# A two-layer transformer block on one core: squares summed elementwise on VectorE, small TensorE products issued in groups of four

## The chip, the core and the metric
The kernel runs on one core of a Trainium2 chip. Its time is device microseconds of one execution. Three runs of the kernel before took 1551.24, 1543.52 and 1548.08 us, so the median is 1548.08.

## The reference, cut to what matters
A sequence of 512 tokens of width 1024 goes through two layers. Layer 0 has a mixer of two kinds of attention and a dense feed-forward. Layer 1 has a mixer of sparse attention and eight experts. Every mixer and every feed-forward reads a normalized x, scaled and shifted by a modulation, and its result is multiplied by a third modulation before it is added to x:

```python
sh_m, sc_m, g_m, sh_f, sc_f, g_f = ada_modulation(c, ada_w, ada_b)   # six rows of 1024 from silu(c) @ ada_w
h = rms_norm(x, norm_mix) * (1 + sc_m) + sh_m
x = x + g_m * mix
h = rms_norm(x, norm_ffn) * (1 + sc_f) + sh_f
logits = (t @ router_w).astype(jnp.float32) + router_b     # layer 1: 8 experts, the best two of each token
```

rms_norm needs, for every token, the sum of the squares of its 1024 features.

## The kernel before, in words
x is held as xT: features on the partitions, 8 tiles (k) of [128, 512 tokens]. All is float32. Large products are made of three products of rounded parts (mm3, lines 306 to 308): a weight block is loaded into a raw tile by SP's queue (wraw, line 288), rounded by ScalarE (line 297, wh) and the rest is taken by VectorE (line 299, wl). In the mixers there are three tiles of each kind. An instruction order is made by a planner from the program, by its own estimates of cost; each engine then runs its queue in that order.

Four places compute a norm. The first is at the very start, from the loaded xT. The other three are inside down, the products that end a mixer or a feed-forward: layer 0's output product (eout, from 248 us), the second half of layer 0's feed-forward (edn, from 626 us) and layer 1's output product (oout, from 914 us). down makes one feature tile of x at a time (24 or 30 products), updates xT by VectorE (line 496), and hands the tile before it to Norms.add. ScalarE squares it (line 417). For k below 6 TensorE sums the square over its 128 partitions by a product with a [128, 32] tile of ones, into one of four quarters of a bank (line 420); the quarters are copied, transposed and reduced at k = 5 and 6 (lines 423, 428, 430). The last two squares are summed by token directly: the square is the stationary operand and a column of ones moves (line 433). rstd ends with rsqrt_of.

Two more things are multiplied in small pieces. ada makes one modulation from 16 products [128, 32] x [128, 512] of a column of silu(c), spread over 32 columns, with a weight block (line 346): all products of a column group go to the same quarter of the bank, two blocks of weights make a pair of k-tiles. It runs twice: for modulation 1 of layer 0 at the start, with loads into tiles of its own, and for modulation 2 inside the first mixer, as a generator that is advanced by `fill(later, NA)` behind each of the first pieces of attention, through wraw's tiles. The other modulations are summed by VectorE (ada_vector, lines 368 and 370) and need TensorE only for the sum over partitions (line 374). During layer 0's output product, VectorE sums modulations 3 and 4 in this way, five steps for each tile, from loads in SP's queue. In layer 1's output product logits(k) adds a tile's part of the router's logits (line 1039), one product for each k, in the quarter k % 4. Layer 0's feed-forward and the experts are not touched.

Of the kernel before, what the change touches and what calls it, by code (L numbers as in the profile page):

```python
# [19 lines left out]
P = 128  # L20
# [22 lines left out]
# ---------------------------------------------------------------- host layout  # L43

def _tiles(w, nk, nc):
    """[K, N] -> [K/(nk*128), N/nc, 128, nk*nc], one contiguous block for each tile."""
    k, n = w.shape
    a = w.reshape(k // (nk * P), nk, P, n // nc, nc).transpose(0, 3, 2, 1, 4)
    return a.reshape(k // (nk * P), n // nc, P, nk * nc)


def _in_blocks(w, widths):
    """[1024, N] -> flat blocks for each column group: [128, 8*width], or two [128, 4*width] for a wide one."""
# [7 lines left out]
def _runs(nk):  # L61
    """Runs of k-tiles that share a block of a product with nk of them."""
    if nk <= 8:
        return [nk]
    return [-(-nk // 2), nk // 2]


def _down_blocks(w, groups):
    """[K, 1024] -> flat blocks: for each row group, each 128 columns, each run of k-tiles."""
# [11 lines left out]
def _gate_up_blocks(g, u):  # L81
    """Two [1024, N] -> column groups of 128, in turn gate and up."""
# [5 lines left out]
def _expert_blocks(g, u):  # L88
    """Two [1024, 1408] -> for each column group of THIRDS, each pair of k-tiles, gate and up: [128, 2*width]."""
# [11 lines left out]
def _ada_blocks(w):  # L101
    """[1024, 6144] -> [3 groups of 2048 columns][4 pairs of k-tiles][4 x 512 columns] blocks [128, 2*512]."""
# [53 lines left out]
# ---------------------------------------------------------------- the kernel  # L156
# [8 lines left out]
NA = 2  # L165
# [4 lines left out]
class Blocks:  # L170
    """Hands out consecutive blocks of [128, n] from a flat DRAM array [1, length]."""
# [10 lines left out]
def build(tc, I, out, dbg=None, stop=99):  # L182
# [19 lines left out]
    def temps(n):  # L202
        """The [128, 512] scratch tiles of a phase."""
# [8 lines left out]
    def prob_tiles(n):  # L212
        """The tiles of a phase for the exponentials of the scores."""
# [17 lines left out]
    def banks(**tags):  # L231
        """The PSUM banks of a phase: how many for each use."""
# [5 lines left out]
    # ---- inputs that everything waits for  # L238
# [10 lines left out]
    # ---- constants  # L249
# [21 lines left out]
    # tri[k, q] = 1 for q >= k  # L271
# [4 lines left out]
    # ---- streaming of weights  # L276
# [3 lines left out]
    def weights(raw, high, low):  # L280
        """The tiles of a phase for loaded weights, their high and their low parts."""
# [9 lines left out]
    def wkeep(blocks, nk, ncol):  # L291
        """The next block of weights, [128, nk, ncol]: (loaded, high, low)."""
# [17 lines left out]
    # ---- adaLN modulation  # L310
# [6 lines left out]
    def ada_blocks(layer, which):  # L317
        """The blocks of one of the six modulations: its two column groups' pairs of k-tiles."""
# [3 lines left out]
    def ada_columns(pt, layer, which):  # L322
        """The sums of the column groups of modulations, each on its 32 partitions, to their columns."""
        n = 2 * len(which)
# [5 lines left out]
        pc = pc.rearrange("p (b g r) -> p g b r", b=4, g=n)[:, :, :, 0]  # L330
        for i, w in enumerate(which):
            m = mods[layer, w] = cst.tile([P, KT], F32, name=f"mod{layer}{w}")
            v = V_ADA + 48 * layer + 8 * w
            V.tensor_add(m.rearrange("p (g b) -> p g b", b=4), pc[:, 2 * i:2 * i + 2],
                         vec[:, v:v + 8].rearrange("p (g b) -> p g b", b=4))

    def ada(layer, which, load=wraw, tag="mm"):
        """One of the six modulations, [128, 8]; a generator with a step for each load."""
        src = ada_blocks(layer, which)
        pt = bank(tag, "ada")  # L340
        for kp in range(4):
            for g in range(2):
                raw = load(src(g, kp), 1024)
                for j in range(2):
                    k = 2 * kp + j
                    T.matmul(pt[32 * g:32 * g + 32, :], cb[:, k], raw[:, j * 512:(j + 1) * 512], start=k == 0,
                             stop=k == KT - 1, tile_position=(0, 32 * g))
                yield
# [1149 lines left out]
```

## Time and profile before
| | |
|---|---|
| runs, us | 1543.52, 1548.08, 1551.24 |
| span of the profiled execution, us | 1543.3 |
| mean granted TensorE clock | 0.979 |
| TensorE busy | 1462.0 us, 95% |
| VectorE busy | 1038.0 us, 67% |
| ScalarE busy | 744.3 us, 48% |
| ones-products of the squares (line 420) | 24, in 48 instructions, 24.2 us busy |
| products of ada (line 346) | 32, in 64 instructions, 23.3 us busy |
| router products (line 1039) | 8, in 16 instructions, 7.2 us busy |

The profile is of one execution, and all times in it are microseconds from the start of its span. Nothing is shown of that execution's time outside the span. A float32 product stands in the trace as two matmul instructions. An engine's busy time does not say that it sets the end; the chain of waits does, and the busy time of a single stage.

### The profile page before, as it was taken

The page shows a single profiled execution, that of the slowest core. Times are in us where ns is not written, and L with a number is a line of the kernel's source. Part 1 is how long each engine was busy: PE and PEld are TensorE (multiplying, and loading weights), DVE is VectorE, ACT ScalarE, POOL GpSimd, SP SyncE. Part 2 cuts the span into 40 slices and gives each one's busy share as a digit, 9 for nine tenths or more (in the row PEclk, how much of TensorE's full clock was granted, in tenths as well). Part 3 has the DMA queues.
Part 4 walks back from the last instruction along what each step waited for, and adds up shares of the span by engine and source line. Part 5 has one row for each costly group of instructions (what it writes and reads, how often), then busy time and mean ns, then how long its engine had stood idle before and what let it go on. Part 6 is the DMA issues. An engine that isn't in the chain of part 4 may idle for free.

```text
span 1543.3 us, 23799 instructions
## 1 busy us (share of the span) xinstructions
PE 1462.0 (95%) x8659; PEld 1088.3 (71%) x8659; DVE 1038.0 (67%) x1968; ACT 744.3 (48%) x1252; POOL 149.9 (10%) x165
## 2 busy tenths in 40 slices
PE   7999999999999999999976999999999999999994
PEld 3766776677788878767854676776767777777773
DVE  5845577766574357347899852686677897897784
ACT  5444463332222222235444851665555675675672
POOL 1000000011110001003552000101100100010010
PEclk9999999999999999999998999999999999999997
DMA  8443325466674346333241101676878898798791
GB/s 313 147 129 104 102 84 181 173 205 211 194 233 154 109 129 211 90 96 90 81 116 40 42 28 56 245 252 206 289 234 275 289 367 249 269 386 247 265 390 59
DMA packets 84606, 283.26 MB, mean 184 GB/s; under 512 B 10488, under 2 KB 11272, under 8 KB 84480
## 3 DMA queue, kind: packets, MB, share of 16 engines
q1 hardware_dynamic: 70608, 233.87, 44.6%
q0 software_dynamic: 13872, 47.78, 10.4%
q8 instruction: 70, 1.15, 0.3%
q14 instruction: 56, 0.46, 0.1%
HBM read 261.28 MB, written 11.29 MB: 177 GB/s over the span
## 4 chain that ended last, share of the span: by engine, by line
PE 77%; DVE 9%; DMA 3%; issue 2%; ACT 2%; SPq 0%; POOL 0%; DVEq 0%; ACTq 0%; POOLq 0%
PE pj L306 6%; PE pj L308 6%; PE pj L307 6%; PE dn L306 5%; PE dn L307 5%; PE dn L308 5%; PE v L1310 4%; PE g L1303 3%; PE u L1304 3%; PE u L1303 3%; PE g L1305 3%; PE u L1305 3%; PE g L1304 3%; PE o L658 2%; DMA side<-in_oada 2%
## 5 line engine op out<-in xcount | busy, mean ns | idle before, releaser
L297 ACT CAST wh<-raw 128x1024 fp32r<-128x1024 f32 (+2 forms) x404 | 398.9, 993 | 459.8 <-PE dn L307 127.4
L299 DVE TENSOR_TENSOR wl<-raw,wh 128x1024 fp32r<-128x1024 f32 (+2 forms) x394 | 448.7, 1150 | 161.7 <-ACT wh L297 156.6
L306 PE MATMUL pj<-h,wh 128*128 128x512 f32 x560 | 225.4, 404 | 3.3 <-ACT h L457 3.2
L308 PE MATMUL pj<-h,wl 128*128 128x512 f32 (+1 forms) x560 | 224.1, 401 | 0.1
L307 PE MATMUL pj<-h,wh 128*128 128x512 f32 (+1 forms) x560 | 223.2, 399 | 0.1
L370 DVE SCALAR_TENSOR_TENSOR acc<-side,sc,acc 128x512 f32<-128x512 f32 x140 | 103.5, 750 | 46.2 <-DMA side<-in_oada 39.8
L306 PEld LDWEIGHTS pj<-h,wh 128*128 128x128 f32 x560 | 106.1, 190 | 35.3 <-ACT h L457 3.7
L308 PEld LDWEIGHTS pj<-h,wl 128*128 128x128 f32 (+1 forms) x560 | 106.7, 191 | 26.6 <-issue 1.1
L307 PEld LDWEIGHTS pj<-h,wh 128*128 128x128 f32 (+1 forms) x560 | 106.1, 189 | 25.8 <-issue 1.1
L582 PE MATMUL s<-kd,qs 128*128 128x256 f32 (+2 forms) x152 | 59.6, 395 | 27.3 <-DVE st L629 17.9
L1303 PE MATMUL g<-wh,xe 128*128 128x512 f32 (+1 forms) x192 | 79.3, 413 | 1.2 <-ACT xe L1295 1.2
L496 DVE SCALAR_TENSOR_TENSOR xT<-dn,mod,xT 128x512 f32<-128x512 f32 x32 | 24.0, 750 | 80.1 <-PE dn L308 80.1
L1303 PE MATMUL u<-wh,xe 128*128 128x512 f32 (+1 forms) x192 | 72.8, 379 | 0.0
L1304 PE MATMUL u<-wl,xe 128*128 128x512 f32 (+1 forms) x192 | 72.7, 379 | 0.0
L1305 PE MATMUL g<-wh,xe 128*128 128x512 f32 (+1 forms) x192 | 72.4, 377 | 0.0
L1304 PE MATMUL g<-wl,xe 128*128 128x512 f32 (+1 forms) x192 | 72.3, 376 | 0.0
L1305 PE MATMUL u<-wh,xe 128*128 128x512 f32 (+1 forms) x192 | 72.2, 376 | 0.0
L634 ACT ACTIVATE p<-p,st 128x128 f32<-128x128 f32 (+3 forms) x96 | 53.3, 557 | 36.8 <-DVE st L632 35.2
L306 PE MATMUL dn<-hid,wh 128*128 128x512 f32 x176 | 70.3, 399 | 0.0
L308 PE MATMUL dn<-hid,wl 128*128 128x512 f32 x176 | 69.7, 396 | 0.0
L307 PE MATMUL dn<-hid,wh 128*128 128x512 f32 x176 | 69.2, 393 | 0.0
L1310 PE MATMUL v<-raw,xf 128*32 128x128 f32 x1760 | 67.3, 276 | 0.0
(414 smaller groups left out, 2723.6 us busy)
## 6 DMA issues: line engine op xcount, KB each, us to landing
raw<-in_xgu SPq DMA_DIRECT2D x128, 512.0 KB, 5.8
raw<-in_xdn SPq DMA_DIRECT2D x88, 512.0 KB, 4.9
side<-in_oada POOLq DMA_DIRECT2D x48, 512.0 KB, 4.4
raw<-in_xgu SPq DMA_DIRECT2D x64, 384.0 KB, 5.0
raw<-in_egu SPq DMA_DIRECT2D x44, 512.0 KB, 3.5
side<-in_eada SPq DMA_DIRECT2D x24, 512.0 KB, 5.3
raw<-in_oin SPq DMA_DIRECT2D x16, 512.0 KB, 3.6
raw<-in_ein SPq DMA_DIRECT2D x13, 512.0 KB, 3.6
```

The source lines that it names most:

```text
L297: A.copy(wh[:, :n], raw[:, :n])
L299: (G if stream["turn"] % 8 in blocks.pool else V).tensor_sub(wl[:, :n], raw[:, :n], wh[:, :n].bitcast(F32))
L306: T.matmul(out_, wh, xh, start=start, stop=False)
L307: T.matmul(out_, wh, xl, start=False, stop=False)
L308: T.matmul(out_, wl, xh, start=False, stop=stop)
L370: V.scalar_tensor_tensor(s, r, sc[:, k:k + 1], s, op0=ALU.mult, op1=ALU.add)
L582: T.matmul(o[:, :nk], q, kd[:, jk, 0, k0:k0 + nk], start=True, stop=False)
L634: A.activation(ps_[j][:, :nk], ps_[j][:, :nk], AF.Exp, bias=st[:, 1, j:j + 1], scale=SCALE, accum_out=st[:, 2, j:j + 1])
L1303: T.matmul(o, x[0], wh, start=first, stop=False)
L1304: T.matmul(o, x[0], wl, start=False, stop=False)
L1305: T.matmul(o, x[1], wh, start=False, stop=last)
L1310: T.matmul(o[32 * j:32 * j + 32], x[2], w[:, j * width:(j + 1) * width], start=first, stop=last, tile_position=(0, 32 * j), skip_group_che ...
```

## The change: what it does
- Norms.add squares tile 0 into an accumulator (acc). The squares 1 to 6 are added to it elementwise by VectorE. At k = 6 the accumulator, at k = 7 the last square, is summed by token as the last two squares were before. The ones-products, the copy, the transposes and the reduction are gone.
- ada loads the two column groups' blocks of a pair of k-tiles, then issues four products, each to its own quarter of the bank; a modulation's column is then the sum of two quarters, which ada_columns makes with halves=2. A step of the generator now holds two loads, and NA goes from 2 to 1.
- logits(k) does nothing but at k = 3 and 7, where it issues the four products of k - 3 to k.
- Docstrings and comments are dropped.

```diff
-NA = 2
+NA = 1
-    def ada_columns(pt, layer, which):
-        n = 2 * len(which)
+    def ada_columns(pt, layer, which, halves=1):
+        n = 2 * len(which) * halves
...
-        pc = pc.rearrange("p (b g r) -> p g b r", b=4, g=n)[:, :, :, 0]
+        pc = pc.rearrange("p (b g h r) -> p g b h r", b=4, h=halves, r=32)[:, :, :, :, 0]
...
+            part = pc[:, 2 * i:2 * i + 2, :, 0]
+            if halves > 1:
+                part = t512("ada_s")[:, :8].rearrange("p (g b) -> p g b", b=4)
+                V.tensor_reduce(part, pc[:, 2 * i:2 * i + 2], axis=AX.X, op=ALU.add)
+            V.tensor_add(mg, part, vec[:, v:v + 8].rearrange("p (g b) -> p g b", b=4))
...
         for kp in range(4):
+            raws = [load(src(g, kp), 1024) for g in range(2)]
             for g in range(2):
-                raw = load(src(g, kp), 1024)
                 for j in range(2):
-                    k = 2 * kp + j
-                    T.matmul(pt[32 * g:32 * g + 32, :], cb[:, k], raw[:, j * 512:(j + 1) * 512], start=k == 0,
-                             stop=k == KT - 1, tile_position=(0, 32 * g))
-                yield
-        ada_columns(pt, layer, (which,))
+                    q = 32 * (2 * g + j)
+                    T.matmul(pt[q:q + 32, :], cb[:, 2 * kp + j], raws[g][:, j * 512:(j + 1) * 512], start=kp == 0,
+                             stop=kp == 3, tile_position=(0, q))
+            yield
+        ada_columns(pt, layer, (which,), 2)
...
         def add(self, k):
+            if k == 0:
+                self.acc, self.tok = t512("ssqa"), aux("ssqt")
+                A.activation(self.acc, xT[:, 0], AF.Square)
+                return
             sq = t512("sq")
             A.activation(sq, xT[:, k], AF.Square)
-            if k < 6:
-                g = k % 4
-                T.matmul(self.rows[32 * g:32 * g + 32, :], ones32, sq, start=k < 4, stop=k > 1, tile_position=(0, 32 * g))
-                if k == 5:
-                    self.s4 = t512("ssq4")
-                    V.tensor_copy(self.s4, self.rows)
-                return
-            if k == 6:
-                pt = aux("ssqT")
-                for b in range(NT):
-                    T.transpose(pt[:, b * P:(b + 1) * P], self.s4[:, b * P:(b + 1) * P], identf)
-                self.ss = sm.tile([P, NT], F32, name="ss")
-                V.tensor_reduce(self.ss, pt.rearrange("p (b g r) -> p b g r", b=NT, g=4)[:, :, :, 0], axis=AX.X, op=ALU.add)
-                self.tok = aux("ssqt")
+            if k < KT - 1:
+                V.tensor_add(self.acc, self.acc, sq)
+                if k < KT - 2:
+                    return
+                sq = self.acc
             for b in range(NT):
                 T.matmul(self.tok[:, b:b + 1], sq[:, b * P:(b + 1) * P], ones32[:, 0:1], ...)
...
                 def logits(k):
-                    g = k % 4
-                    T.matmul(lg[32 * g:32 * g + 32, :], arw[:, k], xT[:, k], start=k < 4, stop=k >= 4,
-                             tile_position=(0, 32 * g))
+                    for g in range(4) if k % 4 == 3 else ():
+                        T.matmul(lg[32 * g:32 * g + 32, :], arw[:, k - 3 + g], xT[:, k - 3 + g], start=k < 4, stop=k >= 4,
+                                 tile_position=(0, 32 * g))
```

## Rows read from the trace of the kernel before

**Rows 1.** The page's part 4: the chain that ended last, share by engine
```profile
PE 77%; DVE 9%; DMA 3%; issue 2%; ACT 2%; SPq 0%; POOL 0%; DVEq 0%; ACTq 0%; POOLq 0%
```

**Rows 2.** Four stretches: us, then each engine's busy time, granted clock, DMA share, GB/s
```profile
100.00:248.00 148.00, 148.00 (x805) 101.84 (x804) 92.24 (x259) 82.44 (x228) 2.68 (x5) 0.99 0.32 97
250.90:284.60 33.70, 33.70 (x131) 22.85 (x130) 29.39 (x41) 7.92 (x10) 1.07 (x2) 1.00 0.77 269
629.40:685.20 55.80, 55.80 (x224) 39.76 (x223) 17.13 (x22) 14.81 (x22) 0.00 (x0) 1.00 0.31 89
925.10:970.80 45.70, 45.70 (x170) 28.99 (x171) 10.10 (x12) 7.57 (x10) 0.00 (x0) 1.00 0.17 58
```

**Rows 3.** The chain, 100 to 250 us: start, us, what; one of five, one of three
```profile
110.77 0.98 PE ada L346 x2
...
196.88 1.83 PE ada L346 x4
```

**Rows 4.** TensorE in order, 84 to 102 us: start, us, what, idle before and releaser
```profile
90.02 2.76 PE L346 MATMUL ada<-raw,cb 128*32 128x512 f32 x10
...
99.00 0.39 PE L582 MATMUL s<-kd,qs 128*128 128x256 f32 x1 [3.47 <-DVE st L629]
```

**Rows 5.** TensorE in order, 290 to 306 us
```profile
291.32 0.60 PE L428 MATMUL ssqT<-identf,ssq 128*128 128x128 f32 x4
...
292.64 1.06 PE L374 MATMUL ada<-acc,ones 128*32 128x512 f32 x8
```

**Rows 6.** VectorE in order, the feed-forward's last product
```profile
629.36 0.75 DVE L496 SCALAR_TENSOR_TENSOR xT<-dn,mod,xT 128x512 f32<-128x512 f32 x1 [2.10 <-PE dn L308]
...
636.35 0.75 DVE L496 SCALAR_TENSOR_TENSOR xT<-dn,mod,xT 128x512 f32<-128x512 f32 x1 [2.10 <-PE dn L308]
...
644.49 0.75 DVE L496 SCALAR_TENSOR_TENSOR xT<-dn,mod,xT 128x512 f32<-128x512 f32 x1 [2.10 <-PE dn L308]
```

**Rows 7.** VectorE in order, the start
```profile
19.02 4.86 DVE L740 TENSOR_TENSOR xn<-xT,rstd 128x512 f32<-128x512 f32 x8
```

**Rows 8.** TensorE in order, the end of the feed-forward's last product
```profile
686.69 1.05 PE L433 MATMUL ssqt<-ones,sq 128*128 128x1 f32 x8 [0.28 <-ACT sq L417]
```

**Rows 9.** VectorE in order, layer 1's output product
```profile
919.53 0.75 DVE L496 SCALAR_TENSOR_TENSOR xT<-dn,mod,xT 128x512 f32<-128x512 f32 x1 [5.05 <-PE dn L308]
...
925.11 0.75 DVE L496 SCALAR_TENSOR_TENSOR xT<-dn,mod,xT 128x512 f32<-128x512 f32 x1 [3.50 <-PE dn L308]
...
932.72 0.75 DVE L496 SCALAR_TENSOR_TENSOR xT<-dn,mod,xT 128x512 f32<-128x512 f32 x1 [5.53 <-PE dn L308]
```

**Rows 10.** VectorE in order, layer 0's output product
```profile
264.51 0.75 DVE L496 SCALAR_TENSOR_TENSOR xT<-dn,mod,xT 128x512 f32<-128x512 f32 x1 [1.54 <-PE dn L308]
...
271.26 0.75 DVE L496 SCALAR_TENSOR_TENSOR xT<-dn,mod,xT 128x512 f32<-128x512 f32 x1 [0.97 <-PE dn L308]
...
278.02 0.75 DVE L496 SCALAR_TENSOR_TENSOR xT<-dn,mod,xT 128x512 f32<-128x512 f32 x1 [1.04 <-PE dn L308]
...
281.71 1.22 DVE L299 TENSOR_TENSOR wl<-raw,wh 128x1024 fp32r<-128x1024 f32 x1
```

**Rows 11.** Groups by line and shape: busy us, mean ns of one, idle before
```profile
L299 DVE TENSOR_TENSOR wl<-raw,wh 128x1024 fp32r<-128x1024 f32 x295 | 356.9, 1221 | 100.4 <-ACT wh L297 96.8
L297 ACT CAST wh<-raw 128x1024 fp32r<-128x1024 f32 x305 | 317.7, 1049 | 333.1 <-issue 82.8 <-PE pj L307 74.1 <-PE dn L307 54.0
```

**Rows 12.** SP's issues in order, layer 0's output product
```profile
267.38 0.42 SPq L288 DMA_DIRECT2D raw<-in_eout  x1
```

**Rows 13.** TensorE in order, the start
```profile
18.84 8.53 PE L346 MATMUL ada<-st,cb 128*32 128x512 f32 x30
```

**Rows 14.** SP's issues in order, the start
```profile
4.86 16.25 SPq L745 DMA_DIRECT2D st<-in_eada  x8
```

**Rows 15.** The page's part 6: KB each, median us from issue to landing
```profile
raw<-in_ein SPq DMA_DIRECT2D x13, 512.0 KB, 3.6
```

**Rows 16.** One stretch behind layer 0's output product: columns as in rows 2
```profile
299.70:305.30 5.60, 5.60 (x14) 4.29 (x15) 5.60 (x9) 3.29 (x5) 0.00 (x0) 0.51 0.00 0
```

More of the change, by code (lines that the diff above doesn't have):

```diff
@@ L329, in ada_columns @@
             T.transpose(pc[:, b * 32 * n:(b + 1) * 32 * n], rows[:32 * n, b * P:(b + 1) * P], identf[:32 * n, :32 * n])
-        pc = pc.rearrange("p (b g r) -> p g b r", b=4, g=n)[:, :, :, 0]
+        pc = pc.rearrange("p (b g h r) -> p g b h r", b=4, h=halves, r=32)[:, :, :, :, 0]
         for i, w in enumerate(which):
             m = mods[layer, w] = cst.tile([P, KT], F32, name=f"mod{layer}{w}")
+            mg = m.rearrange("p (g b) -> p g b", b=4)
             v = V_ADA + 48 * layer + 8 * w
-            V.tensor_add(m.rearrange("p (g b) -> p g b", b=4), pc[:, 2 * i:2 * i + 2],
-                         vec[:, v:v + 8].rearrange("p (g b) -> p g b", b=4))
+            part = pc[:, 2 * i:2 * i + 2, :, 0]
[3 more added lines that the diff above has]
+            V.tensor_add(mg, part, vec[:, v:v + 8].rearrange("p (g b) -> p g b", b=4))
     def ada(layer, which, load=wraw, tag="mm"):
@@ L408, in build @@
     class Norms:
-        def __init__(self):
-            self.rows, self.tok = aux("ssq"), None
         def add(self, k):
+            if k == 0:
+                self.acc, self.tok = t512("ssqa"), aux("ssqt")
+                A.activation(self.acc, xT[:, 0], AF.Square)
+                return
             sq = t512("sq")
             A.activation(sq, xT[:, k], AF.Square)
-            if k < 6:
-                g = k % 4
-                T.matmul(self.rows[32 * g:32 * g + 32, :], ones32, sq, start=k < 4, stop=k > 1, tile_position=(0, 32 * g))
-                if k == 5:
-                    self.s4 = t512("ssq4")
-                    V.tensor_copy(self.s4, self.rows)
-                return
-            if k == 6:
-                pt = aux("ssqT")
-                for b in range(NT):
-                    T.transpose(pt[:, b * P:(b + 1) * P], self.s4[:, b * P:(b + 1) * P], identf)
-                self.ss = sm.tile([P, NT], F32, name="ss")
-                V.tensor_reduce(self.ss, pt.rearrange("p (b g r) -> p b g r", b=NT, g=4)[:, :, :, 0], axis=AX.X, op=ALU.add)
-                self.tok = aux("ssqt")
+            if k < KT - 1:
[3 more added lines that the diff above has]
+                sq = self.acc
             for b in range(NT):
-                T.matmul(self.tok[:, b:b + 1], sq[:, b * P:(b + 1) * P], ones32[:, 0:1], start=k == 6 and b == 0,
-                         stop=k == 7 and b == NT - 1, skip_group_check=True)
+                T.matmul(self.tok[:, b:b + 1], sq[:, b * P:(b + 1) * P], ones32[:, 0:1], start=k == KT - 2 and b == 0,
+                         stop=k == KT - 1 and b == NT - 1, skip_group_check=True)
         def rstd(self):
-            V.tensor_add(self.ss, self.tok[:, :NT], self.ss)
-            return rsqrt_of(self.ss, NT)
+            ss = sm.tile([P, NT], F32, name="ss")
+            V.tensor_copy(ss, self.tok[:, :NT])
+            return rsqrt_of(ss, NT)
     ended = []
```

## The prediction, made before the changed kernel was run
> **What bounds the kernel now.** I began with the chain of work that ended last: 77% of the span is TensorE [rows 1]. Time taken from TensorE is time gained, then, unless another engine becomes late. Since the change touches four stages, I next asked for the busy time of each engine in those stages [rows 2]. In the first mixer (100 to 248 us) and in the three products that feed the norms, TensorE is busy for the whole stretch at the full clock, 2.4 GHz. VectorE is busy for 92 of 148 us in the mixer, 17 of 56 in the feed-forward's last product and 10 of 46 in layer 1's output product. The exception is layer 0's output product, 29.4 of 33.7 us: there VectorE also sums four modulations. The reader should carry two things from these rows: VectorE has room for additions in three of the four stages, and in the fourth hardly any.
>
> **Modulation 2 in the first mixer.** The 16 products of ada(0, 2) stand on the chain as eight pieces, five of one product (0.98 us) and three of two (1.83 us): 10.4 us for 11 products [rows 3]. The other five ran together in 2.76 us, just before TensorE waited 3.47 us for a softmax anyway [rows 4], so they cost nothing. A product is two instructions, so "x2" is one product. What four products to four quarters cost when they are issued together is shown by the sums of ada_vector: x8 in 1.06 us [rows 5], as much as one. After the change there are four such groups. One meets the same slack, three stay on the path: 3.2 us, gain 7.2. Least, with all four on the path: 6.2. Most, with a second in slack: 8.3. The doubled rows add a little reduction on VectorE and wider transposes, all long before the modulation is used.
> The row has its four products share one stationary operand; ours have four. The Trainium skill, "TensorE: Matmul & The Clock Gate", Part 3, measured less than the full factor: 2.38 times for three column tiles. By its factor a group would cost 1.06 x 3 / 2.38, an estimate of 1.3 us, and the whole sum would be about 1 us smaller. I take the row.
>
> **The feed-forward's last product.** Ends of a feature tile are marked by the update of xT: 629.36, 636.35, 644.49 [rows 6]. The first gap, 6.99 us, has no sum of squares in it, the second, 8.14 us, has one. So each ones-product costs 1.15 us with what it disturbs; six of them, 6.9 us. Six additions on VectorE take their place. They cost 0.61 us each by the nearest row, eight elementwise products of this shape in 4.86 us [rows 7], beside an engine busy 17 of 56 us: nothing on the path. The acc tile keeps one of the six scratch tiles, and the squares need at most two or three others. At the end TensorE already waits 0.28 us for the last square [rows 8], so the transposes that go from in front of it bring nothing there; the additions up to k = 6 end before that square.
>
> **Layer 1's output product.** Here each tile has a ones-product and a router product: 7.61 us from 925.11 to 932.72, against 5.58 us for the tile before them, 24 products alone [rows 9]. The six pairs cost 6 x 2.03 = 12.2 us. Of the router's products one group of four comes back inside the stream, 1.06 us and 0.2 of disturbance (1.15 less the bare 0.98); the second group stands at the end, where two products stood. Gain 10.9 us. If two groups are on the path, 9.7; if the four transposes that go (at most 0.60, [rows 5]) are felt at the end, 11.5.
>
> **Layer 0's output product.** A tile takes 6.75 us (264.51 to 271.26 [rows 10]); without its ones-product 5.58, as in layer 1 [rows 9]: 7.0 us on TensorE. But VectorE becomes late. Before the split of the last weight block at 281.71 it idled 1.54, 0.97 and 1.04 us, always for TensorE [rows 10]; these 3.55 us go when TensorE is faster, and five additions of 0.61, 3.05 us, come in. The split therefore ends at about 282.4 instead of 282.9 (1.22 us long [rows 11]). The last tile began at 291.32 - 5.58 = 285.7 [rows 5]; it can now begin at 282.4, no earlier. Gain 3.3 us instead of 7.0. SP speaks the same way: the next to last block's load is issued at 267.38, behind loads of modulation weights [rows 12], which wait for tiles that VectorE frees. The four transposes go from a chain in which the last square is late anyway (0.4). I take 3.7; the ends are 0, if splits are queued behind more sums, and 7.4.
>
> **The start.** ada(0, 1) ends at 18.84 + 8.53 = 27.4 us [rows 13], already with two quarters in flight (15 products in 8.53 us). Its last load is issued before 21.1 [rows 14]. With the 3.6 us of the nearest landing [rows 15] it is there at 24.7; a group of 1.06 ends at 25.8. That would gain 1.6 us, from which the wider transposes and a reduction take back up to 0.6 (four of full width are 0.60 [rows 5]). Against it stands the clock. The ones-products of the first norm, TensorE's first work, go, and the groups wait for pairs of loads. After a similar lull the granted clock was 0.51, the lower level of 1.2 GHz, from 299.70 to 305.30: 14 products in 5.60 us [rows 16], where 0.233 us each (5.58 / 24) would be 3.3. So the first projections could lose 2.3 us. Ends: 1.6 gained, 2.9 lost. I take 0, near the middle.
> A rule speaks against the change here: the Trainium skill, the same page, Part 1, says that the throttled state is the default and activity releases it. The rows above agree; by the rule the start would lose, and that is the last rival below.
>
> **The sum.** 7.2 + 6.9 + 10.9 + 3.7 + 0 = 28.7 us. The profiled execution's span is 1543.3, about the fastest run (1543.52); it becomes 1514.6. The median of the runs lies 4.8 above the span, and I assume the same for the new kernel: 1519.
>
> **Rivals.**
> 1. TensorE alone decides everywhere. For it: every stretch of rows 2 has TensorE fully busy. Against: VectorE's 29.4 of 33.7. Then 8.3 + 6.9 + 11.5 + 7.4 + 1.6 = 35.7 us: 1512.
> 2. Only layer 1 and the feed-forward pay: the mixer's waits between softmax and products move into the time set free, and layer 0's output product becomes VectorE's and SP's. For it: the 3.47 us wait in the mixer and the SP row. Against: 148.0 of 148.0 busy. 6.9 + 10.9 = 17.8: 1530.
> 3. The change doesn't do what it says: groups with four different stationary operands run one after another. Then the mixer gains nothing and layer 1 only its ones-products, 6 x 1.17 = 7.0; with 6.9 and 3.7 that is 17.6: 1530. Against: the five products in 2.76 us already overlap, 0.55 us each.
> 4. Slower: the mixer starves for loaded weights. There are three raw tiles; a pair for modulation 2 holds two of them from its landing until TensorE reaches the group, and the SP queue stops at the next load, with copies of keys and rope's swaps behind it. A block then has to be loaded (3.6 [rows 15]), rounded (1.05) and split (1.22 [rows 11]), 5.9 us in series, not in advance. At four pairs the change is slower from 28.7 / 4 = 7.2 us a pair, that is one such series and 1.3 us of a key copy behind it; at 9 us a pair, half a series more, it is 1548 - 29 + 36 = 1555. Against: TensorE waited only 3.47 us long once in this stretch, and three rounded and split blocks stand in front of it.
> 5. The clock stays low at the start: 2.9 lost there: 1522.
>
> **How the numbers follow.** The forecast has a chance of 0.50, the rivals, in order, 0.15, 0.14, 0.05, 0.06 and 0.10. What a measurement can tell from no change is about 0.5%, so faster is below 1540.3. The forecast, rivals 1 and 5 lie below it; of rivals 2 and 3, whose times are uncertain by some 10 us from the planner's new order, I leave a part to "same": faster 0.88, same 0.06, slower 0.06. The range: down to 1507 (rival 1 and a median that falls with the span), up to 1537 (rivals 2 and 3 and 7 us).
>
> **What would show it.** In the profile after: xT updates 7.0 us apart in the feed-forward's last product and 5.6 in layer 1's output product, with one gap of about 6.8; groups x8 of some 1.06 us, four in the mixer and two for the router; additions of about 0.69 us on VectorE; in layer 0's output product TensorE waiting for a split in its last two tiles, so an average tile near 6.2. Tiles of 5.6 there mean rival 1, groups of 3.5 us rival 3, loads that keep TensorE waiting between 100 and 240 us rival 4. The prediction is wrong if the mixer from 100 us to the first xT update is not about 7 us shorter.

## The result and the profile after

The changed kernel took 1521.66 us, the median of four runs (1519.0 to 1523.86), beside 1549.66 for the kernel before. The ratio is 0.983, with a 95% interval of 0.980 to 0.986. The profiled execution took 1520.32 us with a span of 1518.6, which is 24.7 us less than the span of before. The forecast was 1519 us, and a span 28.7 us shorter.

I cut both spans at the same landmarks: the first bias product behind the first projections (end of "start"), the first and last update of xT in each of the three products that feed a norm, and the first product of the stage behind each of them. "Forecast" is the gain that the prediction gave.

| stage | before, us | after, us | gain | forecast |
|---|---|---|---|---|
| start | 50.86 | 54.68 | -3.82 | 0 |
| first mixer | 197.59 | 192.02 | 5.57 | 7.2 |
| layer 0's output product and what follows | 51.24 | 46.89 | 4.35 | 3.7 |
| feed-forward, up to its last product | 329.67 | 328.16 | 1.51 | |
| its last product and what follows | 62.07 | 55.09 | 6.98 | 6.9 |
| layer 1's mixer | 228.10 | 226.99 | 1.11 | |
| layer 1's output product and what follows | 63.83 | 52.52 | 11.31 | 10.9 |
| experts | 559.94 | 562.25 | -2.31 | |
| sum | 1543.3 | 1518.6 | 24.7 | 28.7 |

The chain that ended last has the same shares as in [rows 1]:

```profile
PE 77%; DVE 9%; DMA 3%; issue 2%; ACT 2%; SPq 0%; POOL 0%; DVEq 0%; ACTq 0%; POOLq 0%
```

The four stretches of the kernel after, with the columns of [rows 2] (us, busy time of TensorE, its weight loads, VectorE, ScalarE and GpSimd, granted clock, DMA share, GB/s):

```profile
100.00:246.70 146.70, 145.10 (x810) 101.61 (x811) 92.81 (x262) 82.29 (x229) 2.69 (x5) 0.99 0.33 101
249.26:280.24 30.98, 28.50 (x121) 22.40 (x120) 29.45 (x43) 8.09 (x10) 0.46 (x1) 1.00 0.76 267
621.75:670.63 48.88, 48.88 (x213) 39.45 (x211) 20.50 (x27) 14.91 (x22) 0.00 (x0) 1.00 0.35 102
909.42:944.13 34.71, 34.71 (x155) 27.15 (x153) 13.19 (x16) 7.56 (x10) 0.00 (x0) 1.00 0.24 77
```

The last two stretches are still TensorE's from end to end, and shorter. In the second, TensorE now has 2.5 us without work, while VectorE is busy for 29.45 of 30.98 us: the limit has moved there. The first is no longer full either.

VectorE in order, in the feed-forward's last product and in layer 1's output product (start, us, line, operation, and in brackets the idle time before it with what ended it); these answer to [rows 6] and [rows 9]:

```profile
628.73 0.75 DVE L495 SCALAR_TENSOR_TENSOR xT<-dn,mod,xT 128x512 f32<-128x512 f32 x1 [2.09 <-PE dn L308]
...
630.18 0.69 DVE L426 TENSOR_TENSOR ssqa<-ssqa,sq 128x512 f32<-128x512 f32 x1
...
635.72 0.75 DVE L495 SCALAR_TENSOR_TENSOR xT<-dn,mod,xT 128x512 f32<-128x512 f32 x1 [2.10 <-PE dn L308]
...
920.60 0.75 DVE L495 SCALAR_TENSOR_TENSOR xT<-dn,mod,xT 128x512 f32<-128x512 f32 x1 [2.91 <-PE dn L308]
...
926.18 0.75 DVE L495 SCALAR_TENSOR_TENSOR xT<-dn,mod,xT 128x512 f32<-128x512 f32 x1 [2.86 <-PE dn L308]
...
932.96 0.75 DVE L495 SCALAR_TENSOR_TENSOR xT<-dn,mod,xT 128x512 f32<-128x512 f32 x1 [4.05 <-PE dn L308]
```

The tiles are 6.99 us apart, and 5.58 with one gap of 6.78. VectorE waits for TensorE before every update, so an addition of 0.69 us costs nothing here. The longer gap holds the router's first group, eight instructions in the time of one product; the second stands at the end:

```profile
926.07 1.07 PE L1038 MATMUL lg<-xT,arw 128*32 128x512 f32 x8
...
944.81 1.17 PE L1038 MATMUL lg<-xT,arw 128*32 128x512 f32 x8
```

TensorE in order, the products of modulation 2 in the mixer of after (compare [rows 3] and [rows 4]; two instructions are one product):

```profile
92.29 1.07 PE L352 MATMUL ada<-raw,cb 128*32 128x512 f32 x8
93.68 1.04 PE L352 MATMUL ada<-raw,cb 128*32 128x512 f32 x2 [0.33 <-DMA raw<-in_eada]
100.49 0.38 PE L581 MATMUL s<-kd,qs 128*128 128x256 f32 x1 [2.78 <-DVE st L628]
111.78 1.06 PE L352 MATMUL ada<-raw,cb 128*32 128x512 f32 x6
116.82 1.04 PE L352 MATMUL ada<-raw,cb 128*32 128x512 f32 x2 [0.60 <-DMA raw<-in_eada]
125.81 1.06 PE L352 MATMUL ada<-raw,cb 128*32 128x512 f32 x6
149.62 1.04 PE L352 MATMUL ada<-raw,cb 128*32 128x512 f32 x2
160.80 1.06 PE L352 MATMUL ada<-raw,cb 128*32 128x512 f32 x6
```

Four groups of four were expected. The planner made pieces of 5, 3, 1, 3, 1 and 3 products: it pulls one product of each next pair ahead. Five pieces stand on the path where the prediction has three.

TensorE at the start of after (compare [rows 13]):

```profile
14.02 1.87 PE L431 MATMUL ssqt<-ones,ssqa 128*128 128x1 f32 x8 [14.02 <-DVE ssqa L426]
15.74 1.84 PE L431 MATMUL ssqt<-ones,sq 128*128 128x1 f32 x8
...
19.95 1.08 PE L445 MATMUL rstd<-identf,rs_r 128*128 128x128 f32 x4 [0.52 <-DVE rs_r L411]
...
31.91 0.98 PE L306 MATMUL first<-h,early 128*128 128x512 f32 x3 [1.73 <-ACT h L766]
```

TensorE's first work is now at 14.02 us, and eight one-column sums take 1.87 us, where they took 1.05 in the feed-forward's last product [rows 8]. In the kernel before, rstd's products began at 18.11 us and the first projection at 29.76.

Layer 0's output product of after, VectorE in order (answers to [rows 10]):

```profile
270.49 0.49 DVE L374 TENSOR_SCALAR acc<-side,sc 128x512 f32<-128x512 f32 x1 [1.12 <-DMA side<-in_eada]
...
272.21 0.75 DVE L495 SCALAR_TENSOR_TENSOR xT<-dn,mod,xT 128x512 f32<-128x512 f32 x1
...
273.53 1.22 DVE L299 TENSOR_TENSOR wl<-raw,wh 128x1024 fp32r<-128x1024 f32 x1
```

TensorE there, the two products that wait for this block's rounding and for its split; ScalarE's rounding; and SP's load of the block, the next to last one (answers to [rows 12]):

```profile
273.11 0.50 PE L306 MATMUL dn<-o,wh 128*128 128x512 f32 x1 [1.52 <-ACT wh L297]
...
274.81 0.50 PE L308 MATMUL dn<-o,wl 128*128 128x512 f32 x1 [0.96 <-DVE wl L299]
```
```profile
272.01 1.04 ACT L297 CAST wh<-raw 128x1024 fp32r<-128x1024 f32 x1 [4.56 <-DMA raw<-in_eout]
```
```profile
265.20 0.42 SPq L288 DMA_DIRECT2D raw<-in_eout  x1
```

The larger of TensorE's two waits, 1.52 us, is for the rounding, and ScalarE had waited for the load. In this profile the block comes late as a whole: it is loaded late, rounded, and split 0.5 us after that.

From 250 to 280 us the 1.12 us for a load of a modulation's weights is VectorE's only idle time but for 0.32 at the end. Four updates of xT in a row don't wait for TensorE any more, as those in [rows 10] did.

### The profile page after: what moved, and what is told of

Read it like the earlier page. It is cut to its first block, busy times and chain, and to the rows that moved or that the text cites. A ratio compares the mean times of both kernels' runs of the same rounds, so it can differ in the third digit from the quotient of the medians.

```text
span 1518.6 us, 23687 instructions
## 1 busy us (share of the span) xinstructions
PE 1428.2 (94%) x8595; PEld 1084.8 (71%) x8595; DVE 1048.3 (69%) x1986; ACT 745.4 (49%) x1252; POOL 150.5 (10%) x165
## 4 chain that ended last, share of the span: by engine, by line
PE 77%; DVE 9%; DMA 3%; issue 2%; ACT 2%; SPq 0%; POOL 0%; DVEq 0%; ACTq 0%; POOLq 0%
PE pj L306 7%; PE pj L307 7%; PE pj L308 7%; PE dn L306 4%; PE dn L308 4%; PE dn L307 4%; PE v L1309 4%; PE g L1302 3%; PE g L1304 3%; PE u L1303 3%; PE u L1302 3%; PE g L1303 3%; PE u L1304 3%; PE o L657 2%; PE yv L1309 2%
## 5 line engine op out<-in xcount | busy, mean ns | idle before, releaser
L376 DVE SCALAR_TENSOR_TENSOR acc<-side,sc,acc 128x512 f32<-128x512 f32 x140 | 103.5, 750 | 41.5 <-DMA side<-in_oada 36.4
L581 PE MATMUL s<-kd,qs 128*128 128x256 f32 (+2 forms) x152 | 60.0, 397 | 24.7 <-DVE st L628 17.0
L1309 PEld LDWEIGHTS v<-raw,xf 128*32 128x32 f32 x1760 | 49.3, 109 | 21.4 <-issue 12.1
```

The source lines that it names most:

```text
L376: V.scalar_tensor_tensor(s, r, sc[:, k:k + 1], s, op0=ALU.mult, op1=ALU.add)
L581: T.matmul(o[:, :nk], q, kd[:, jk, 0, k0:k0 + nk], start=True, stop=False)
L1309: T.matmul(o[32 * j:32 * j + 32], x[2], w[:, j * width:(j + 1) * width], start=first, stop=last, tile_position=(0, 32 * j), skip_group_che ...
```

## Experiments

### Each part alone

Three kernels are the kernel before with one part of the change: the class Norms of the kernel after (norms_only), its ada with NA = 1 (ada_only), or its logits (router_only). Each diff is that part of the diff above, here its core:

```diff
-                T.matmul(self.rows[32 * g:32 * g + 32, :], ones32, sq, ...)               # norms_only
+                V.tensor_add(self.acc, self.acc, sq)
...
+            raws = [load(src(g, kp), 1024) for g in range(2)]                            # ada_only
...
+                    for g in range(4) if k % 4 == 3 else ():                             # router_only
```

> The kernel before with the new Norms alone. Theory (each stage pays for itself): the feed-forward's last product 7.0 us shorter, layer 1's output product 6 x 1.16 = 7.0, layer 0's output product about 4.3 (VectorE becomes late there), the start 2 us longer, because the sums by token of the first norm then run at the lower clock: about 16 us less than before, tiles of 7.0 us in the feed-forward's last product. Rival (the start's loss belongs to the modulation's pairs of loads, not to the norm): start unchanged, 18 us less.

> The kernel before with ada's groups of four alone. Theory: the first mixer 5.6 us shorter, the start 1.7 us longer (wider columns, lower clock in the first projections): about 4 us less than before. Rival (the whole loss of 3.8 us at the start comes from the pairs of loads): under 2 us less.

> The kernel before with the router's products in groups of four alone. Theory: layer 1's output product loses six single products at 2.03 - 1.15 = 0.88 us each and gets one group of about 1.2: 4.1 us less than before, tiles of 6.7 us with one of about 8. Rival (a group of four different stationary operands is not concurrent, 3.4 us): 1.8 us less, one tile of about 10.

| kernel | median, us | ratio to before, interval |
|---|---|---|
| norms_only | 1530.14 | 0.987, 0.984 to 0.990 |
| ada_only | 1545.06 | 0.998, 0.996 to 1.000 |
| router_only | 1543.72 | 0.996, 0.995 to 0.998 |

The three gains, 1.3 + 0.2 + 0.4%, add up to 1.9%, and the whole change has 1.7% (1.4 to 2.0): by the runs, no effect of one part on another can be told. By stages of the profiles: the norms gain 7.0 us in the feed-forward's last product, 5.2 in layer 1's output product and 4.1 in layer 0's. The router's groups gain 4.3 in layer 1's output product, and ada 3.0 in the mixer. Both edits of layer 1's output product together gain 11.0 there, more than 5.2 + 4.3: a pair of a ones-product and a router product costs 2.03 us in a tile, either alone 1.17 (tiles of 6.75 us in both single kernels), so that the first one taken out brings only 0.86. In this stage, then, the two edits do help each other, by 1.5 us.

The profiles of norms_only and router_only are near their theories (tiles of 7.0, and of 6.75 with one of 7.62 us). ada_only misses its own in the mixer, 3.0 us for 5.6; the section on the mixer shows why such a difference can't be taken from one profile.

### The mixer: are the groups split to the change's harm?

tight_groups starts with the block that lands last and binds the four products to each other:

```diff
+            head = None
-            for g in range(2):
+            for g in (1, 0):
                 for j in range(2):
                     q = 32 * (2 * g + j)
-                    T.matmul(pt[q:q + 32, :], cb[:, 2 * kp + j], raws[g][:, j * 512:(j + 1) * 512], ...)
+                    with ExitStack() as tight:
+                        if head is not None:
+                            tight.enter_context(tc.high_priority(offset=3000))
+                            tight.enter_context(tc.issue_after(head.ins))
+                        m_ = T.matmul(pt[q:q + 32, :], cb[:, 2 * kp + j], raws[g][:, j * 512:(j + 1) * 512], ...)
+                    head = head or m_
```

> The changed kernel with the four products of ada bound together in TensorE's order, the later load's first. In the changed kernel the planner splits the groups of the mixer into 5, 3, 1, 3, 1, 3 products. Theory (each piece costs one product's time on the path, however many it holds): three pieces on the path instead of five, the mixer 2 us shorter than in the changed kernel, 26 us less than the profiled run of before. Rival (a whole group has to wait for both loads and TensorE idles for them): the same time as the changed kernel, with waits for in_eada in front of the groups.

It took 1521.18 us, a ratio of 0.981 (0.978 to 0.984), which the changed kernel's interval overlaps. The mixer of its profile is 2.35 us shorter than in the changed kernel. TensorE in order there; the fourth group, at 158.51, is alike:

```profile
92.38 1.06 PE L357 MATMUL ada<-raw,cb 128*32 128x512 f32 x8
94.56 0.47 PE L306 MATMUL pj<-h,wh 128*128 128x512 f32 x1 [1.12 <-DVE qs L564]
100.63 0.39 PE L587 MATMUL s<-kd,qs 128*128 128x256 f32 x1 [2.58 <-DVE st L634]
106.84 1.07 PE L357 MATMUL ada<-raw,cb 128*32 128x512 f32 x8
112.57 0.39 PE L587 MATMUL s<-kd,qs 128*128 128x256 f32 x1 [1.17 <-DVE st L634]
123.14 1.07 PE L357 MATMUL ada<-raw,cb 128*32 128x512 f32 x8
124.96 0.66 PE L652 MATMUL tr<-identf,p 128*128 128x128 f32 x4 [0.76 <-ACT rr L600]
```

Now there are three groups on the path, as forecast, but TensorE waits elsewhere: 1.12 us for a query, 1.17 and 0.76 for a softmax. With 2.58 and two small waits that is 6.26 us behind 84 us, where the kernel before waited 3.47 and the changed one 4.17. What the groups save comes back as waits for VectorE and ScalarE: 7.2 less 2.8 is 4.4 us. For the changed kernel, five pieces (5.3 us) in place of 10.4 save 5.1, less 0.7 of new waits, also 4.4.

The difference of 2.35 us between the two profiles has another cause: the granted clock. Two places of the mixer, each behind a wait of TensorE, 62 to 68 us (behind 1.88 us for a copy of v) and 98 to 104 us (behind the softmax), of the kernels before, after and tight_groups, in this order; columns as above. The first wait ends at 62.26 us in the kernel before and at 66.09 and 66.18 in the other two, where the clock stays at 1.00 behind it too:

```profile
62.00:68.00 6.00, 5.74 (x35) 5.74 (x36) 5.74 (x10) 1.53 (x4) 0.00 (x0) 0.72 0.73 152
98.00:104.00 6.00, 5.00 (x20) 3.64 (x21) 2.01 (x12) 3.08 (x10) 0.00 (x0) 0.72 0.21 85
```
```profile
62.00:68.00 6.00, 4.12 (x35) 3.91 (x35) 5.65 (x11) 4.06 (x8) 0.00 (x0) 1.00 0.36 75
98.00:104.00 6.00, 3.51 (x16) 2.65 (x17) 2.93 (x12) 4.30 (x10) 0.00 (x0) 0.83 0.31 107
```
```profile
62.00:68.00 6.00, 4.12 (x35) 3.92 (x34) 5.69 (x10) 3.96 (x8) 0.00 (x0) 1.00 0.34 71
98.00:104.00 6.00, 3.42 (x21) 2.74 (x20) 3.35 (x15) 3.59 (x8) 0.00 (x0) 1.00 0.37 115
```

A mean of 1.00 is 2.4 GHz throughout, 0.72 a mixture of the two levels. To take this out I added up, for stretches of 2 us, TensorE's busy time times (1 - granted clock); I call the sums dips. They, and the stages' lengths without them, in us:

| kernel | dips: start, from 28 us | mixer, to 84 us | mixer, from 84 us | layer 0's output product and what follows | start less dips | mixer less dips |
|---|---|---|---|---|---|---|
| before | 0.00 | 1.62 | 1.72 | 0.17 | 50.86 | 194.25 |
| router_only | 1.48 | 1.58 | 1.52 | 0.00 | 51.88 | 194.46 |
| before_warm | 1.65 | 1.72 | 3.15 | 0.00 | 50.96 | 193.03 |
| norms_only | 1.66 | 1.71 | 3.28 | 0.04 | 53.09 | 193.65 |
| after | 1.68 | 0.00 | 1.70 | 0.09 | 53.00 | 190.32 |
| ada_only | 1.66 | 1.71 | 3.13 | 0.75 | 51.06 | 189.79 |
| start_old_norm | 1.39 | 1.67 | 0.00 | 2.96 | 51.28 | 189.62 |
| pool_adds | 0.00 | 1.68 | 2.75 | 2.87 | 52.68 | 190.83 |
| side_on_pool | 1.67 | 1.70 | 2.83 | 2.51 | 52.67 | 190.15 |
| eout_no_adds | 1.50 | 1.59 | 0.00 | 1.30 | 51.76 | 189.39 |
| warm_products | 0.00 | 1.72 | 3.09 | 1.26 | 49.81 | 189.33 |
| warm_eleven | 1.58 | 1.64 | 2.88 | 1.37 | 49.70 | 189.84 |
| tight_groups | 2.96 | 0.00 | 0.00 | 2.86 | 51.82 | 189.67 |
| tight_warm | 2.56 | 1.63 | 0.00 | 3.03 | 50.65 | 190.50 |

The kernels that are not yet described follow below. A stretch that straddles the end of a stage is counted whole, which makes the last of the four columns of dips up to 0.8 us too large. The table leaves out what lies before 28 us. There the record has dips of 1.7 us in the kernel before and 3.1 in router_only and none in the changed kernel, whose slow first sums stand at a recorded 1.00; so starts less dips can be compared to about 1 us only.

Less the dips, the mixer has a mean of 193.85 us in the four profiles with the old modulation (the first four, 193.0 to 194.5), 189.9 in the eight with the change's own groups (189.3 to 190.8) and 190.1 in the last two, with the groups kept together. So the mixer's gain is 3.9 us, 5.57 was that and a dip of 1.6 that the changed kernel's profile happened not to have, and keeping the groups together brings nothing that shows. The count of pieces and waits above gives 4.4 us; the 0.5 between the two is within the spread of the profiles.

### The start

warm_products gives TensorE work before the first norm, products of ones that nothing reads. start_old_norm keeps the whole change but takes the first norm from the class of the kernel before. before_warm is the kernel before with the same twelve products.

```diff
+        still = t512("still")
+        V.memset(still, 1.0)
+        warm = bank("mm", "warm")
+        for i in range(12):
+            T.matmul(warm[:32], ones32, still, start=i == 0, stop=i == 11, tile_position=(0, 0))
         norms = Norms()
```
```diff
-        norms = Norms()
+        norms = OnesNorms()
         for k in range(KT):
             norms.add(k)
```

> The changed kernel with 12 products of ones on a constant tile put in front of the first norm, where TensorE has no work; their result isn't read. Theory (the sums by token of the first norm take 1.87 and 1.84 us because TensorE's clock is at its lower level after it did nothing): the two take about 0.95 us each, rstd's rows are made 1.8 us sooner, the first pairs of modulation weights are freed sooner and the start is 1.4 to 1.9 us shorter than in the changed kernel. Rival (the start is later because VectorE's last addition stands behind five small casts and ends at 13.97, and because of the wider columns): the sums are as slow as before or the start moves by under 0.5 us.

> The changed kernel with ones-products on TensorE in the first norm alone; the three norms inside down stay as changed. Theory (TensorE is idle there, so its products cost nothing and keep its clock up): the start 1.4 to 2 us shorter than in the changed kernel, 1.9 us sooner rows of rstd, the rest as it was. Rival (loads bound the start): rows of rstd sooner, the first projections not.

> The kernel before, with the twelve products of ones on a constant tile ahead of the first norm, and nothing of the change. Theory: the low clock at the start is not the change's alone; the kernel before starts TensorE with ones-products that wait for squares, and whether its first projections run at the high level differs between executions (0.23 us spacing in its own profile, 0.43 in that of the kernel with only the router's groups). Then the products gain it 0 to 1 us against its own profiled start of 50.86 and about 2 us against its usual one: the ratio is 0.997 to 0.999. Rival: only the changed kernel lacks early activity, and the twelve products gain nothing here or delay the first ones-products: the start is 50.9 or later and the ratio 1.000 or above.

warm_products took 1517.83 us (0.980, 0.976 to 0.984) and start_old_norm 1515.94 (0.978, 0.976 to 0.981). before_warm took 1549.89 (1.002, 1.0004 to 1.004), so its rival held: the old start isn't helped. There the twelve products stood in front of the ones-products, and rstd's products came at 23.39 us, not at 18.11. In the profile of start_old_norm the start is 2.0 us shorter than in the changed kernel, as its theory has it, but rstd's products come at 18.94 us, 1.0 sooner and not 1.9.

In its one profile warm_products made the start 4.87 us shorter than in the changed kernel, with the clock at 1.00 throughout, and I took this for the cause of the start's 3.82. That was half right. Less dips the start takes 50.9 us in the kernel before, 53.0 in the changed one, 51.3 with the old norm and 49.8 with the twelve products. So 2.1 of the 3.82 us are the change's in this pair of profiles. Over all profiles it is rather 1.3: the old start has 50.9 and 51.9 us (before, router_only), the changed one 51.8 to 53.1 with a mean of 52.6 (norms_only, after, pool_adds, side_on_pool, eout_no_adds). TensorE's sums come at 14.02, behind the last addition, and run long; in the kernel before they began no earlier (13.90), but all sixteen took 1.84 us. The other 1.7 are a dip in the first projections that the kernel before has in some profiles and not in others: router_only starts with the same instructions, and its start took 53.36 us, not 50.86.

### Both edits together

tight_warm is tight_groups with the twelve products.

> Both edits that helped on their own, in one kernel: the twelve products of ones at the start and modulation 2's groups kept together in the mixer. Theory: the two gains are in different stages and add up. Measured against the changed kernel they were 4.87 us at the start and 2.35 us in the mixer, so the span goes from 1518.6 to some 1511.5 and the median of the runs to 1512 to 1515; in the trace the first projections run at 0.23 us spacing from their first on, and the mixer has four groups of x8 in one piece each. Rival: part of the two gains is the difference between one execution and another at the start and in the mixer (up to 2 us each in stages that no edit touched), and the ratio to the kernel before stays where either edit alone put it, at 0.980.

It took 1520.21 us: 0.983 (0.981 to 0.986). The sum of the two gains, 1511.5, did not come; the rival foretold no gain over either alone, and even that is a little better than what was measured. Its start in the trace, by stretches:

```profile
28.00:32.00 4.00, 2.29 (x7) 1.68 (x8) 2.49 (x6) 3.13 (x6) 0.00 (x0) 0.50 1.03 410
32.00:36.00 4.00, 4.00 (x14) 3.12 (x13) 4.00 (x7) 4.00 (x7) 0.00 (x0) 0.64 0.62 246
```

In this program too the sums took 1.05 us, but the clock had fallen before the first projections (0.65 from 24 to 26 us, 0.50 from 26 to 28): TensorE had waited 2.62 and 1.52 us for loads of the modulation, and then 1.42 for h. Early products shorten the sums; they do not decide the level of the first projections.

The last kernel has eleven products, so that the last one ends before VectorE's last addition (the diff is `range(11)`).

> The changed kernel with eleven products of ones on a constant tile ahead of the first norm, one fewer than in the earlier try, where the twelfth ended 1.1 us after VectorE's last addition. The products keep the first norm's sums and rstd at the short durations (sums 1.05 us instead of 1.87). Theory, after a count of TensorE's time below the full clock by stage: the start's own time, without those dips of the clock, goes from 53.0 us in the changed kernel to 49 to 50, and nothing behind it changes by the edit; dips of 1.4 to 3 us stay, at places that differ between executions (first projections, 62 to 66 us, the wait for the softmax near 100 us, layer 0's output product), so that the span may come anywhere from 1514 to 1518 and the ratio to the kernel before at 0.978 to 0.981, with the start's sums at 14.0 to 16 us in any case. Rival: the twelve products' gain of 4.87 us at the start was no more than a dip that did not occur in that one execution: the sums are short here too, but rstd's products begin at 19.5 or later as in the changed kernel, and the ratio is 0.983 or above.

```profile
13.88 1.05 PE L431 MATMUL ssqt<-ones,ssqa 128*128 128x1 f32 x8 [0.61 <-DVE ssqa L426]
...
18.48 1.01 PE L445 MATMUL rstd<-identf,rs_r 128*128 128x128 f32 x4
...
29.09 1.32 PE L306 MATMUL first<-h,early 128*128 128x512 f32 x3 [1.42 <-ACT h L771]
```

It took 1518.49 us, a ratio of 0.980 (0.978 to 0.983). The theory held: sums of 1.05 us at 13.88, the first projection at 29.09 instead of 31.91, and a start of 51.28 us, or 49.7 less its dip of 1.58. That the kernel is faster than the changed one by the 2 to 3 us that this is worth can't be told: the intervals overlap.

### Layer 0's output product

pool_adds moves this stage's additions to GpSimd. side_on_pool lets GpSimd's queue issue the loads of modulations 3 and 4. eout_no_adds leaves five of the six additions out, so that layer 0's second norm is of too few features; only this stage of it is read, as the numbers behind it change the experts' work.

```diff
-                V.tensor_add(self.acc, self.acc, sq)
+                self.eng.tensor_add(self.acc, self.acc, sq)      # pool_adds: eng = G in this stage
```
```diff
-    ... ada_vector(0, (3, 4), av, nc.sync, NS)
+    ... ada_vector(0, (3, 4), av, G, NS)                         # side_on_pool
```
```diff
-                V.tensor_add(self.acc, self.acc, sq)
+                if self.adds or k == KT - 2:                     # eout_no_adds: adds = False in this stage
+                    V.tensor_add(self.acc, self.acc, sq)
```

> The changed kernel with the additions of layer 0's output product on GpSimd instead of VectorE. Theory (VectorE bounds this stage: six additions of 0.61 us beside the sums of modulations): 3 us of its 39.1 go, tiles nearer to 5.6 us; GpSimd takes 1.4 us for each, which nobody waits for. Rival (the next to last block of weights is late in any case, its load stands in SP's queue until 265 us): under 1 us.

> The changed kernel with the loads of modulations 3 and 4 in GpSimd's queue instead of SP's. Theory (SP's queue holds back the last two blocks of layer 0's output weights behind loads that wait for VectorE): these blocks are loaded long before 265 us and the splits are not late; together with VectorE's work 1 to 2 us of 39.1 go. Rival (VectorE alone): the splits stay where they stand, 0 us.

> Leaves out five of the six additions of squares in layer 0's output product (so rstd of layer 0's feed-forward is of fewer features); everything else is the changed kernel. Theory: VectorE sets the pace there, and the additions (0.69 us each, 3.45 in all) are what it lacks: the stage from the first to the last xT update goes from 39.14 us to 36 to 37, and the first projection of the feed-forward comes as much earlier. Rival: the loads set it (SP's queue, which reaches the next to last block at 267.85 behind thirteen loads of modulation weights): then the stage stays at 38.5 to 39.2 and TensorE waits as long, for a split that waits for a load.

pool_adds took 1525.09 us (0.984, 0.981 to 0.987), and the stage, from the first to the last update of xT, became 4.61 us longer than in the changed kernel; about half of that is a dip of the clock behind a wait of 4.09 us for a split. GpSimd in order, then VectorE in order beside it:

```profile
265.02 1.72 POOL L429 TENSOR_TENSOR ssqa<-ssqa,sq 128x512 f32<-128x512 f32 x1 [4.54 <-ACT sq L427]
...
277.99 1.46 POOL L429 TENSOR_TENSOR ssqa<-ssqa,sq 128x512 f32<-128x512 f32 x1 [4.40 <-ACT sq L427]
```
```profile
265.52 1.51 DVE L374 TENSOR_SCALAR acc<-side,sc 128x512 f32<-128x512 f32 x1
...
278.24 4.12 DVE L376 SCALAR_TENSOR_TENSOR acc<-side,sc,acc 128x512 f32<-128x512 f32 x4
```

L374 takes 0.48 us when GpSimd is idle, and four of L376 took 3.10 in eout_no_adds:

```profile
270.96 3.10 DVE L376 SCALAR_TENSOR_TENSOR acc<-side,sc,acc 128x512 f32<-128x512 f32 x4
```

Both differences are 1.0 us. So such an addition on GpSimd takes 1.0 us from VectorE, more than the 0.69 us that it costs on VectorE itself. The Trainium skill, "SBUF — State Buffer", in "SBUF: two separate sides", says that the port pair which the two engines share is an exclusive lock, held for a whole instruction, so that the other blocks. The trace agrees: 1.51 us is 0.48 and most of what was left of GpSimd's addition when L374 began (1.22).

side_on_pool took 1518.27 us (0.980, 0.977 to 0.983). With the loads out of SP's queue the stage is 1.12 us shorter than in the changed kernel, but what follows is 4.00 longer: the modulations' sums now come last, TensorE waits 1.52 us for them at 290.30, and behind this wait the clock falls (1.8 us of dip up to the landmark).

In eout_no_adds the stage took 37.88 us, between what the two theories say (36 to 37, and 38.5 to 39.2). TensorE still waits for a split there:

```profile
271.10 0.50 PE L308 MATMUL dn<-o,wl 128*128 128x512 f32 x1 [1.52 <-DVE wl L299]
```

VectorE stands without idle time from 258.65 to 279 us even then: sums of modulations are queued in front of the split. So 3.45 us of additions cost at most 1.3 of the stage. Less dips, the stage takes 38.4 to 39.1 us in the seven profiles that have its instructions as changed (norms_only, after, start_old_norm, the three with products of ones on the changed start, tight_groups); against these the additions cost 0.5 to 1.3, and what side_on_pool gains in the stage is 0.4 to 1.1. VectorE is the limit, as predicted, but through the modulations' sums and their place in its queue more than through the additions. The loads have a part in it: SP's queue reached the next to last block 17.4 us behind the stage's first update of xT here, and 18.5 in the changed kernel (at 265.20 us; 267.85, which the expectation names, is the last block). In three of the seven profiles TensorE waits for the split alone, 2.18 us (start_old_norm, tight_groups, warm_eleven).

## Why the prediction was right, and where it was not

- **The feed-forward's last product** gained 6.98 us (forecast 6.9), with tiles 6.99 us apart. The additions are free, as argued.
- **Layer 1's output product** gained 11.31 us with what follows (10.9). Tiles of 5.58 and one of 6.78 are as forecast; the rest lies in the ends.
- **Layer 0's output product** gained 4.35 us with what follows (3.7, ends 0 and 7.4), and the limit moved to VectorE and to a split for which TensorE waits, as foretold. The average tile was to be near 6.2; the five from 249.26 to 280.24 us have 6.20. Two things were read wrong: VectorE sums two modulations in this stage, not four, and the larger of TensorE's two waits in the profile of after was for the rounding of a late block, which the sum doesn't have.
- **The mixer** was mis-sized: 5.57 us in the two profiles, of which 3.9 are the change's, for 7.2 forecast. By the prediction's own test (about 7 us shorter) this step was wrong. The step that failed is "there are four such groups. One meets the same slack, three stay on the path". The planner left five pieces, and where the groups are held together the time goes into waits for VectorE and ScalarE that TensorE's full queue had hidden. Rival 2's mechanism, waits that move into the time set free, takes 2.8 of the 7.2 us there; in the changed kernel it is two pieces more (2.1) and 0.7 of waits.
- **What a group costs** was right: three products with three stationary operands took 1.06 us, four 1.06 to 1.07, one alone 1.04. Rival 3 falls. The Trainium skill, "TensorE: Matmul & The Clock Gate", Part 3, has a factor of 2.38 for three column tiles; here it is 1.04 x 3 / 1.06, 2.9, and the measurement decides.
- **The start** was to cost nothing, between 1.6 gained and 2.9 lost. Its 3.82 lost lie outside, but 1.7 are a dip in the first projections, as in rival 5, which the old start has as well in other executions (router_only). The change's own 1.3 to 2.1 lie inside, and come from the first norm, not from ada: the old norm brings the start back to 51.3 us less dips, and ada alone leaves it at 51.1. These starts are good to about 1 us, as said at the table. Of the two terms behind the 0, the gain of 1.6 for ada didn't come: its last load was to be issued before 21.1 us, and it was issued at 23.33 in the changed kernel and at 21.42 in ada_only, where the last group ended at 27.05 us, beside 27.4 in the kernel before.
- **The sum.** The terms that were too large (the mixer by 1.6, the start by 3.8) and too small (layer 0's and layer 1's output products, 1.1 together) leave 24.7 us where 28.7 were forecast, with 0.3 from the other stages. The medians of the runs differ by 28.0. That this is so near to 28.7 is luck in part, since two terms missed by 5.4 us together and the two profiles differ by 24.7. The median lay 3.1 us above the profiled span of after, where 4.8 was assumed.

What stays open is which edit of the start is worth keeping: 0.978 with the old norm, 0.980 with eleven or twelve products and 0.983 unedited have overlapping intervals.

## What to carry to other kernels

Price a small product from the distance of two tiles with and without it, in the stage itself: that gave 6.9 and 10.9 us to within half a microsecond. Small products that are to run together must also be issued together, so look at the order that the planner makes of them, and expect part of what they save in a stage full of dependences to come back as waits. Before a difference of one to five microseconds between two profiles is put down to an edit, add up TensorE's time below its full clock in each stage.

## What the runs showed of the hardware that was not expected

- **Dips of the clock come and go between executions.** Behind the same wait of 1.88 us, which ends between 61 and 67 us, the clock fell in twelve of the fourteen profiles (to 0.72 over six us in the kernel before) and stayed at 1.00 in two, after and tight_groups, for the same instructions. What decides it stays open. Most entries of the table are 1.3 to 3.3 us. From 28 us to the end of layer 0's output product a profile has 3.5 to 8.7 us of dips, which is as much as the smaller terms of the prediction. There are more behind it: added up alike, the experts have 3.4 us in the profile of before and 5.1 in that of after, most of the 2.31 us that they seem to lose.
- **The granted clock need not show a slow start.** From 13 to 20 us the profile of after reads 1.00, yet sums take 1.87 us there and 1.05 when products ran before them.
- **GpSimd's elementwise additions** took 1.39 to 1.93 us for what VectorE does in 0.69, and took 1.0 us of VectorE's time as well.
